# Prompt attention of an encoder layer: float32 steps on half of the array become float32r steps on the whole array

## The chip, the cores and the metric

One core of a Trainium2 chip runs the whole layer. The metric is device microseconds of one execution. TensorE (PE) multiplies; a weight load (PEld) comes ahead of every matmul. VectorE (DVE), ScalarE (ACT) and GpSimd (POOL) do the element-wise work, each from an in-order queue; SyncE (SP), ACT and POOL also issue DMAs.

## What is computed

The layer has a SwiGLU block, a mixer and a second SwiGLU block. The change lies in the mixer's attention over the 1024 prompt tokens: 16 query heads on 2 key heads, 64 wide; queries come in chunks of 64, and each chunk sees its own and the two earlier chunks (192 keys). A relative-position bias is added, and each head has a sink that joins the softmax without a value.

```python
s = jnp.einsum('...qhgd,...khd->...hgqk', q, k).astype(jnp.float32) * (HEAD_DIM ** -0.5) + bias
...
p = jax.nn.softmax(jnp.concatenate([s, sink_col], axis=-1), axis=-1)[..., :-1]
return jnp.einsum('...hgqk,...khd->...qhgd', p.astype(v.dtype), v)
...
merged = jax.nn.sigmoid(ga) * (attn @ w_ba) + jax.nn.sigmoid(gb) * (gm @ w_bg)
```

The attention of the 128 sample tokens (8 streams of 16) follows the same formula over cached keys.

## The kernel before

The 1152 tokens are nine tiles of 128, eight of the prompt and one of the samples. Everything runs over tiles 0 to 4 (block 0) and then tiles 5 to 8 (block 1). The large products (`mm3`, lines 254 to 256) split each float32 operand into hi (rounded to float32r) and lo (the rest) and take three float32r steps: hi·hi, hi·lo, lo·hi.

In the mixer, `project` makes queries, keys, values, gates and sigmoids; `attend` runs the attention with steps of another product between its pieces, the *filler*: `second`, the branch of the spatial gate (64 filler steps, each two `mm3`, so 384 float32r steps of half the block's tokens: 320 columns in block 0, 256 in block 1). After that `first` multiplies the attention's result with its weights and merges both branches; the output projection follows.

A *unit* of the attention is one pair of heads p (0 to 7, in the order `P_ORDER`) and one tile of 128 tokens: 8 x 5 = 40 units in block 0; 8 x 3 = 24 prompt units and 16 sample units in block 1. A unit has three parts. `scores`: two products of a pair's 128 query rows with 192 keys over the 64 rows of one head (line 1140, plain float32, 64 of 128 array rows), each followed on DVE by bias and running maximum (line 1143); a small row that bounds the maximum by the sink (1148); on ACT the exponentials with their sums (1151) and that of the sink (1153). `turn`: sum and reciprocal (1157, 1158), the division (1160, two rows), four transposes on PE (1166) and their copy from PSUM (1168, half on ACT, half on DVE). `values`: four float32 products that fill 64 of the 128 output rows each (1179); every two or three tiles the result is split into hi and lo (lines 264 and 265 of `put_split`). For each new unit's scores, the loop emits the turn of the second unit before it and the values of the third, with filler steps between; a scheduler then sets the order on each queue at build time. The weights of the filler are cut into hi (157, ACT) and lo (160, DVE), one pair per eight filler steps. The two halves of each of the filler's results are multiplied with a sigmoid that POOL loads from DRAM (`sig_load`), line 1300 on DVE.

## Time and profile before

| | us |
|---|---|
| median of 3 runs | 2617.04 (2615.02 to 2621.6) |
| span of the profiled execution | 2612.4 |
| PE busy | 2568.4 (98%) |
| DVE busy | 1885.8 (72%) |
| ACT busy | 1365.3 (52%) |
| POOL busy | 178.0 (7%) |
| share of PE in the chain that ended last | 91% |

The page's busy time is the time in which an engine has at least one instruction in flight. Neighbouring instructions of one engine overlap a little, so durations add up to more than busy time. A plain float32 product appears as two MATMUL records. "Idle before" is the engine's idle time just before the instructions of a group, with what ended it.

### The profile page before, as it was taken

To read this page: it belongs to the slowest core of one execution; us is meant where nothing else is said; L and a number is where in the kernel's file an instruction comes from. 1 tells how busy PE (TensorE), PEld (TensorE's weight loads), DVE (VectorE), ACT (ScalarE), POOL (GpSimd) and SP (SyncE) were. 2 spreads that over 40 slices of the span, in tenths; PEclk is the share of its full clock that TensorE was granted. 3 is DMA by queue.
4 is the path that set the end of the run, shared out by engine and by line. 5 is a ranking of instruction groups with operands and counts; after the bars stand their busy time and mean duration, and the time that the engine had idled before them with its cause. 6 is when DMAs were issued, how large, how long until landed. Compare 5 with 4: busy or idle time off the path is not lost.

```text
span 2612.4 us, 43405 instructions
## 1 busy us (share of the span) xinstructions
PE 2568.4 (98%) x16996; PEld 2349.2 (90%) x16996; DVE 1885.8 (72%) x3464; ACT 1365.3 (52%) x2575; POOL 178.0 (7%) x268
## 2 busy tenths in 40 slices
PE   6999999999999999999999999999999999999998
PEld 6999987999978999977989898797999987899986
DVE  6777664788877686666857877788876665688885
ACT  5444553555565555744446567545544454455552
POOL 1000000000210000100200201031000000000030
PEclk9999999999999999999999999999999999999999
DMA  4423322333443224412423444253332323333462
GB/s 123 97 82 97 114 95 95 118 113 98 163 144 116 82 90 148 126 56 65 167 86 113 127 147 132 71 179 120 108 95 81 97 89 109 126 99 113 129 209 81
DMA packets 216333, 293.92 MB, mean 113 GB/s; under 512 B 10824, under 2 KB 168880, under 8 KB 216128
## 3 DMA queue, kind: packets, MB, share of 16 engines
q1 hardware_dynamic: 183312, 212.36, 25.4%
q0 software_dynamic: 18048, 59.36, 7.6%
q10 hardware_dynamic: 14768, 19.43, 2.1%
q8 instruction: 133, 2.18, 0.3%
q14 instruction: 72, 0.59, 0.1%
HBM read 255.72 MB, written 35.39 MB: 111 GB/s over the span
## 4 chain that ended last, share of the span: by engine, by line
PE 91%; DVE 4%; DMA 2%; ACT 1%; issue 1%; SPq 0%; DVEq 0%; ACTq 0%
PE ps L254 28%; PE ps L255 28%; PE ps L256 28%; PE ps L1140 2%; PE ps L1179 2%; PE ps L1166 1%; PE ps L435 1%; DVE wl L160 1%; DMA wr<-in_w_in_dram 1%; DMA wr<-in_ffn_w_up_dram 1%; PE ps L1024 0%; DVE arena_r L265 0%; ACT wh L157 0%; DMA y<-w 0%; PE ps L962 0%
## 5 line engine op out<-in xcount | busy, mean ns | idle before, releaser
L254 PE MATMUL ps<-arena_r,wh 128*128 128x320 f32 (+1 forms) x4160 | 1244.1, 299 | 3.5 <-ACT arena_r L264 1.5
L256 PE MATMUL ps<-arena_r,wl 128*128 128x320 f32 (+1 forms) x4160 | 1229.2, 296 | 5.5 <-DVE wl L160 5.1
L255 PE MATMUL ps<-arena_r,wh 128*128 128x320 f32 (+1 forms) x4160 | 1230.8, 296 | 0.3 <-DVE arena_r L265 0.3
L254 PEld LDWEIGHTS ps<-arena_r,wh 128*128 128x128 f32 x4160 | 783.8, 188 | 16.6 <-issue 9.6
L256 PEld LDWEIGHTS ps<-arena_r,wl 128*128 128x128 f32 x4160 | 782.9, 188 | 11.9 <-DVE wl L160 7.4
L255 PEld LDWEIGHTS ps<-arena_r,wh 128*128 128x128 f32 x4160 | 783.7, 188 | 6.6 <-issue 5.0
L160 DVE TENSOR_TENSOR wl<-wr,wh 128x1024 fp32r<-128x1024 f32 x404 | 503.1, 1246 | 254.7 <-ACT wh L157 246.0
L157 ACT CAST wh<-wr 128x1024 fp32r<-128x1024 f32 x404 | 419.7, 1039 | 214.3 <-PE ps L255 178.8
L254 PE MATMUL ps<-wh,arena_r 128*128 128x512 f32 x936 | 374.9, 401 | 1.0 <-ACT arena_r L264 1.0
L255 PE MATMUL ps<-wl,arena_r 128*128 128x512 f32 x936 | 369.5, 395 | 0.0
L256 PE MATMUL ps<-wh,arena_r 128*128 128x512 f32 x936 | 369.0, 395 | 0.4 <-DVE arena_r L265 0.4
L264 ACT CAST arena_r<-arena 128x640 fp32r<-128x640 f32 (+4 forms) x246 | 158.9, 654 | 267.4 <-PE ps L255 220.3
L265 DVE TENSOR_TENSOR arena_r<-arena,arena_r 128x640 fp32r<-128x640 f32 (+4 forms) x246 | 186.7, 768 | 148.2 <-ACT arena_r L264 143.4
L256 PEld LDWEIGHTS ps<-wh,arena_r 128*128 128x128 f32 x936 | 175.4, 187 | 43.5 <-DVE arena_r L265 0.8
L254 PEld LDWEIGHTS ps<-wh,arena_r 128*128 128x128 f32 x936 | 175.5, 188 | 42.1 <-ACT arena_r L264 1.8
L255 PEld LDWEIGHTS ps<-wl,arena_r 128*128 128x128 f32 x936 | 175.7, 188 | 39.7
L541 DVE TENSOR_TENSOR t<-t,ps 128x320 f32<-128x320 f32 (+1 forms) x384 | 169.6, 446 | 46.1 <-PE ps L256 35.6
L160 DVE TENSOR_TENSOR wl<-arena,wh 128x1024 fp32r<-128x1024 f32 (+1 forms) x130 | 156.4, 1203 | 57.2 <-ACT wh L157 56.5
L545 ACT COPY t<-ps 128x320 f32<-128x320 f32 (+1 forms) x384 | 151.2, 396 | 81.4 <-PE ps L256 80.5
L157 ACT CAST wh<-arena 128x1024 fp32r<-128x1024 f32 (+1 forms) x130 | 134.6, 1035 | 111.2 <-PE ps L255 89.9
L597 ACT ACTIVATE t<-t 128x256 f32<-128x256 f32 (+1 forms) x129 | 57.3, 444 | 169.5 <-DVE t L541 169.4
L157 ACT CAST wh<-gn 128x1024 fp32r<-128x1024 f32 (+1 forms) x65 | 67.5, 1038 | 51.0 <-PE ps L255 42.3
(241 smaller groups left out, 2163.6 us busy)
## 6 DMA issues: line engine op xcount, KB each, us to landing
wr<-in_ffn_w_gate_dram SPq DMA_DIRECT2D x88, 512.0 KB, 4.0
wr<-in_ffn_w_up_dram SPq DMA_DIRECT2D x88, 512.0 KB, 5.0
wr<-in_w_in_dram SPq DMA_DIRECT2D x84, 512.0 KB, 4.9
wr<-in_ffn_w_down_dram SPq DMA_DIRECT2D x40, 1024.0 KB, 5.0
y<-w ACTq DMA_DIRECT2D x38, 256.0 KB, 3.4
arena<-x POOLq DMA_DIRECT2D x19, 512.0 KB, 4.2
arena<-y POOLq DMA_DIRECT2D x17, 512.0 KB, 5.2
x<-arena POOLq DMA_DIRECT2D x16, 512.0 KB, 3.0
```

The costliest lines, as they stand in the source:

```text
L157: nc.scalar.copy(out=self.hi, in_=self.src)
L160: nc.vector.tensor_tensor(out=self.lo, in0=self.src, in1=self.hi.bitcast(F32), op=ALU.subtract)
L254: nc.tensor.matmul(out, lh, rh, start=start, stop=False, skip_group_check=again)
L255: nc.tensor.matmul(out, lh, rl, start=False, stop=False, skip_group_check=again)
L256: nc.tensor.matmul(out, ll, rh, start=False, stop=stop, skip_group_check=again)
L264: nc.scalar.copy(out=hi, in_=src)
L265: nc.vector.tensor_tensor(out=lo, in0=src, in1=hi.bitcast(F32), op=ALU.subtract)
L541: nc.vector.tensor_tensor(out=out, in0=a, in1=b, op=ALU.add)
L545: nc.scalar.copy(out=t, in_=ps)
L597: nc.scalar.activation(out=t, in_=v, func=AF.Silu)
L1140: nc.tensor.matmul(sc, self.q[p % 4][hp, 2 * mi + c].rearrange("p e q -> p (e q)"), k_all[hp, k1 - n:k1], start=True, stop=True)
L1179: nc.tensor.matmul(po[64 * e:64 * e + 64, c0:c0 + P], v_t[:, m - 1 + a, hp], pt[:, a, :, 64 * e:64 * e + 64], start=(a == a0), stop=(a == 1))
```

## The change

Scores and values of the prompt units become float32r steps that use all 128 rows and columns.

- The keys of one head are split into hi and lo, each laid on both halves of the partitions (`keys`, twice per block). The queries of a pair lie as hi on one half and lo on the other (`queries`, once per pair): ACT copies 64 rows, DVE subtracts 64 rows. One step over 128 rows then gives (hi + lo of the queries) times hi of the keys, a second step the same with lo.
- The values lie as hi and lo side by side (128 columns). The transposed probabilities are split with `put_split` into hi (ACT) and lo (DVE), 512 columns each. Four float32r steps of 256 columns give the product with hi in 64 output rows and with lo in the other 64; for each tile ACT copies one half (64 x 256) and DVE adds the halves in two rows (64 x 128).
- Scores are kept negated (queries scaled by -1/8, bias table negated), the running minimum starts at the negated sink, a per-partition column, and the small bounding row goes away. The division is one two-operand row over both chunks (384 columns) in place of two rows of 192, except in tile 0.
- The attention's result is kept in float32 where the spatial gate's part of the merge was kept; that part goes to DRAM over ACT's DMA queue and comes back with the sigmoids in `first` (four loads per feature tile in place of two). All splits of the attention's result come after it, six of them between filler steps.
- The filler steps ahead of the attention and after it are 10 and 8 in place of 6 and 6; `P_ORDER` begins with pair 4.

```diff
+        def keys(self, h):
+            mine, other = (slice(64 * e, 64 * e + 64) for e in (h, 1 - h))
+            src = k_all[mine, self.t0 * P:(self.t0 + self.n_k) * P]
+            hi, lo = self.kr[h]
+            for rows in (mine, other):
+                nc.scalar.copy(out=hi[rows], in_=src)
+            for rows in (mine, other):
+                nc.vector.tensor_tensor(out=lo[rows], in0=src, in1=hi[mine].bitcast(F32), op=ALU.subtract)
+            put_split(self.vr[h][:, :, 0:64], self.vr[h][:, :, 64:128],
+                      v_t[:, self.t0:self.t0 + self.n_k, mine])
+        def queries(self, p):
...
+            nc.scalar.copy(out=t[mine], in_=src)
+            nc.vector.tensor_tensor(out=t[other], in0=src, in1=t[mine].bitcast(F32), op=ALU.subtract)
...
-                    nc.tensor.matmul(sc, self.q[p % 4][hp, 2 * mi + c].rearrange("p e q -> p (e q)"),
-                                     k_all[hp, k1 - n:k1], start=True, stop=True)
-                    seg = pb[:, c, j1 - n:j1]
+                    for a in range(2):
+                        nc.tensor.matmul(sc, qt[:, 2 * mi + c, :], self.kr[h][a][:, k1 - n:k1],
+                                         start=a == 0, stop=a == 1)
+                    seg = pc[:, c, j1 - n:j1]
                     nc.vector.tensor_tensor_reduce(out=seg, in0=sc, in1=bias_of(p)[:, 192 - n:192],
-                                                   scale=1.0, scalar=NEG, op0=ALU.add, op1=ALU.max,
-                                                   accum_out=s[:, c:c + 1])
+                                                   scale=1.0, scalar=nsink_p[:, p:p + 1], op0=ALU.add,
+                                                   op1=ALU.min, accum_out=s[:, 2 + c:3 + c])
                     segs.append(seg)
                 nm = s[:, 2:4]
-                nc.vector.tensor_scalar(out=nm, in0=s[:, 0:2], scalar1=sink, scalar2=-1.0,
-                                        op0=ALU.max, op1=ALU.mult)
...
+                    nc.vector.tensor_tensor(out=both, in0=both, op=ALU.mult,
+                                            in1=rc.unsqueeze(2).broadcast_to([P, 2, 192]))
...
-                for a in range(a0, 2):
-                    (nc.vector.tensor_copy if a else nc.scalar.copy)(out=pt[:, a], in_=ps[:, a])
+                put_split(ph[:, a0:], pl[:, a0:], ps[:, a0:])
...
-                    for e in range(2):
-                        nc.tensor.matmul(po[64 * e:64 * e + 64, c0:c0 + P],
-                                         v_t[:, m - 1 + a, hp], pt[:, a, :, 64 * e:64 * e + 64],
-                                         start=(a == a0), stop=(a == 1))
+                    for pt in (ph, pl):
+                        nc.tensor.matmul(po[:, i * 256:(i + 1) * 256], self.vr[h][:, m - 1 - self.t0 + a, :],
+                                         pt[:, a, :], start=a == a0 and pt is ph, stop=a == 1 and pt is pl)
+                if i == 1 or mi == self.n_p - 1:
+                    for j in range(i + 1):
+                        t = tmp(256)
+                        nc.scalar.copy(out=t[0:64], in_=po[64:128, j * 256:(j + 1) * 256])
...
+                            nc.vector.tensor_tensor(out=out.rearrange("p (n q) -> p n q", q=64),
+                                                    in0=v[0][:, :, e], in1=v[1][:, :, e], op=ALU.add)
...
-                nc.vector.tensor_tensor(out=self.gm[f][:, j * self.w:(j + 1) * self.w], in0=sig, in1=ps,
-                                        op=ALU.mult)
+                nc.vector.tensor_tensor(out=sig[0], in0=sig[0], in1=ps, op=ALU.mult)
+                nc.scalar.dma_start(out=sig_d[1][f][:, j * self.w:(j + 1) * self.w], in_=sig[0])
...
+            for p in P_ORDER[:6]:
+                put_split(*self.attn[p], self.attn_f[p])
+                step()
             run(filler)
-            for p in self.held:
-                put_split(*self.attn[p], self.held[p])
+            for p in P_ORDER[6:]:
+                put_split(*self.attn[p], self.attn_f[p])
...
-    blocks_[0].attend(blocks_[0].second(), 6, 6)
+    blocks_[0].attend(blocks_[0].second(), 10, 8)
```

How the queues change is shown at two places of block 0. In the names, `st` is a unit's column of sums, `w` its scores and probabilities, `ps` a PSUM bank, `gn` the transposed probabilities (after: their hi), `arena_87` float32 and `arena_r_88` float32r places.

DVE before, in the middle of block 0's attention: the units of `st_11612`, `st_11643` and `st_11676`.

```order
L1143 ISA w_10731,st_11643<-ps_11644,arena_87 128x64 [waits PE_49]
L1143 ISA st_11643 128x1
L1143 ISA w_10731,st_11643<-ps_11644,arena_87 128x128 [waits PE_49]
L1157 TENSOR_TENSOR st_11612<-st_11612 128x2 [waits Activation_49]
L1148 TENSOR_SCALAR st_11643<-st_11643,sink_p_124 128x2 [waits DVE_49]
L1158 RECIPROCAL st_11612<-st_11612 128x2 [waits DVE_49]
L1160 TENSOR_SCALAR w_10730<-w_10730,st_11612 128x192 [waits DVE_49]
L1160 TENSOR_SCALAR w_10730<-w_10730,st_11612 128x192
L1157 TENSOR_TENSOR st_11643<-st_11643 128x2 [waits Activation_49]
L1143 ISA w_10732,st_11676<-ps_11677,arena_87 128x192 [waits PE_49]
L1143 ISA st_11676 128x1
L1168 COPY gn_10733<-ps_11663 128x256 [waits Activation_49]
```

The sum of a unit (1157) stands behind its bias rows and the rows of another unit, and a copy of 256 columns ends the unit's turn.

DVE after, in the middle of block 0's attention (units `st_11663`, `st_11698`, `st_11728`; line 1188 is the bias row, 1200 and 1201 sum and reciprocal, 1207 the division, 265 the lo part of the transposed probabilities).

```order
L1188 ISA w_10736,st_11698<-ps_11699,arena_87,nsink_p_126 128x192 [waits PE_49]
L1188 ISA st_11698 128x1
L1207 TENSOR_TENSOR w_10735<-w_10735,st_11663 128x2x192 [waits DVE_49]
L1200 TENSOR_TENSOR st_11698<-st_11698 128x2 [waits Activation_49]
L1201 RECIPROCAL st_11698<-st_11698 128x2 [waits DVE_49]
L1207 TENSOR_TENSOR w_10736<-w_10736,st_11698 128x2x192 [waits DVE_49]
L265 TENSOR_TENSOR arena_r_88<-ps_11718,gn_10737 128x512 [waits Activation_49]
L1188 ISA w_10734,st_11728<-ps_11729,arena_87,nsink_p_126 128x192 [waits PE_49]
L1188 ISA st_11728 128x1
L265 TENSOR_TENSOR arena_r_88<-ps_11748,gn_10737 128x512 [waits Activation_49]
```

The small bounding row is gone, the division is one row, the copy of 256 columns has become a subtraction of 512, and the sum of unit `st_11698` stands one row behind that unit's last bias row.

PE before, in block 0: the end of one unit, the scores of another, and filler.

```order
L1140 MATMUL ps_11757<-arena_87 128x192 [waits DVE_49]
L1166 MATMUL ps_11776<-ident_89,w_10732 128x128 [waits DVE_49] x2
L1166 MATMUL ps_11776<-ident_89,w_10732 128x128 x2
L1179 MATMUL ps_11783<-gn_10733,arena_87 64x128 [waits PE_49]
L1179 MATMUL ps_11783<-gn_10733,arena_87 64x128
L1140 MATMUL ps_11787<-arena_87 128x192
L254 MATMUL ps_11714<-arena_r_88,wh_11279 128x320
L255 MATMUL ps_11714<-arena_r_88,wh_11279 128x320
L256 MATMUL ps_11714<-arena_r_88,wl_11280 128x320
```

Each score call is one plain float32 product over 64 rows, and filler steps follow it.

PE after, in block 0 (1217 the transposes, 1228 the values, 1185 the scores).

```order
L1217 MATMUL ps_11718<-ident_89,w_10734 128x128 [waits DVE_49,PE_49]
L1217 MATMUL ps_11718<-ident_89,w_10734 128x128 [waits Activation_49]
L1217 MATMUL ps_11718<-ident_89,w_10734 128x128 x2
L1228 MATMUL ps_11725<-gn_10737,arena_r_88 128x256 [waits Activation_49]
L1228 MATMUL ps_11725<-arena_r_88 128x256
L1185 MATMUL ps_11729<-arena_r_88 128x192 [waits PE_49]
L1185 MATMUL ps_11729<-arena_r_88 128x192
L1217 MATMUL ps_11748<-ident_89,w_10735 128x128 [waits DVE_49,Activation_49]
L1217 MATMUL ps_11748<-ident_89,w_10735 128x128 [waits Activation_49]
L1217 MATMUL ps_11748<-ident_89,w_10735 128x128 x2
L1228 MATMUL ps_11725<-gn_10737,arena_r_88 128x256 [waits Activation_49]
```

Each score call is now two float32r steps on the whole array, and the value steps wait for ACT (hi) and, for the steps with lo, for DVE.

## Rows read from the trace of the kernel before

**Rows 1.** Windows: stretch, us, busy (count) of PE, PEld, DVE, ACT, POOL; clock, DMA, GB/s
```profile
1060.00:1101.20 41.20, 41.20 (x282) 41.03 (x280) 28.72 (x34) 34.31 (x58) 6.24 (x11) 1.00 0.51 154
1101.20:1244.70 143.50, 143.50 (x924) 103.87 (x924) 95.84 (x434) 68.50 (x256) 10.20 (x19) 1.00 0.20 65
1244.70:1300.00 55.30, 55.30 (x378) 55.30 (x379) 46.12 (x101) 23.58 (x48) 18.86 (x21) 1.00 0.48 161
1602.20:1683.60 81.40, 81.40 (x552) 58.79 (x552) 58.61 (x256) 42.57 (x149) 4.28 (x8) 1.00 0.19 60
1683.60:1730.20 46.60, 46.01 (x414) 38.86 (x414) 32.47 (x141) 22.22 (x101) 10.56 (x30) 1.00 0.31 101
```

**Rows 2.** Groups of PE, block 0's attention: count, busy us, mean ns, idle before
```profile
L254 PE MATMUL ps<-arena_r,wh 128*128 128x320 f32 x111 | 39.9, 359 | 0.0
```

**Rows 3.** The same view, block 1's prompt units
```profile
L254 PE MATMUL ps<-arena_r,wh 128*128 128x256 f32 x67 | 21.4, 319 | 0.0
```

**Rows 4.** Timeline of PE in block 0: start us, length us, instructions
```profile
1099.82 0.31 PE L254 MATMUL ps<-arena_r,wh 128*128 128x320 f32 x1
...
1100.99 0.31 PE L256 MATMUL ps<-arena_r,wl 128*128 128x320 f32 x1
...
1103.04 0.31 PE L256 MATMUL ps<-arena_r,wl 128*128 128x320 f32 x1
1103.28 0.59 PE L1140 MATMUL ps<-arena 64*128 64x192 f32 x2
1103.80 0.41 PE L254 MATMUL ps<-arena_r,wh 128*128 128x320 f32 x1
1104.05 0.31 PE L255 MATMUL ps<-arena_r,wh 128*128 128x320 f32 x1
...
1169.25 0.66 PE L1166 MATMUL ps<-ident,w 128*128 128x128 f32 x4
1169.66 0.39 PE L254 MATMUL ps<-arena_r,wh 128*128 128x320 f32 x1
```

**Rows 5.** Groups of DVE, block 0's attention: count, busy us, mean ns, idle before
```profile
L1143 DVE CUSTOM_DVE_ANT_0 w<-ps,arena 128x192 f32<-128x192 f32 x64 | 22.8, 356 | 22.7 <-PE ps L1140 21.9
L1160 DVE TENSOR_SCALAR w<-w,st 128x192 f32<-128x192 f32 x64 | 18.5, 316 | 0.7
L1148 DVE TENSOR_SCALAR st<-st,sink_p 128x2 f32<-128x2 f32 x40 | 8.9, 224 | 0.1
L160 DVE TENSOR_TENSOR wl<-wr,wh 128x1024 fp32r<-128x1024 f32 x7 | 8.5, 1216 | 0.0
L1300 DVE TENSOR_TENSOR arena<-t,ps 128x320 f32<-128x320 f32 x14 | 6.6, 484 | 1.2 <-PE ps L256 0.8
L1157 DVE TENSOR_TENSOR st<-st 128x2 f32<-128x2 f32 x40 | 6.2, 155 | 2.6 <-ACT st L1153 2.5
L265 DVE TENSOR_TENSOR arena_r<-ps,arena_r 128x384 fp32r<-128x384 f32 x6 | 3.3, 548 | 0.0
L1160 DVE TENSOR_SCALAR w<-w,st 128x64 f32<-128x64 f32 x8 | 2.0, 251 | 0.1
L265 DVE TENSOR_TENSOR arena_r<-arena,arena_r 128x640 fp32r<-128x640 f32 x1 | 0.8, 817 | 0.0
```

**Rows 6.** The same view, block 1's attention
```profile
L265 DVE TENSOR_TENSOR arena_r<-ps,arena_r 128x128 fp32r<-128x128 f32 x4 | 1.1, 285 | 0.4 <-ACT arena_r L264 0.4
```

**Rows 7.** Timeline of ACT and DVE in block 0
```profile
1168.24 0.45 ACT L1151 ACTIVATE w<-w,st 128x192 f32<-128x192 f32 x1
1168.27 0.88 DVE L1300 TENSOR_TENSOR arena<-t,ps 128x320 f32<-128x320 f32 x2
...
1168.68 0.28 ACT L1153 ACTIVATE st<-st,sink_p 128x2 f32<-128x2 f32 x1
```

**Rows 8.** Windows in other stages, where PE has idle time (columns as in Rows 1)
```profile
1490.00:1500.00 10.00, 7.36 (x54) 7.15 (x53) 7.23 (x9) 4.75 (x8) 0.00 (x0) 0.88 0.76 260
1780.00:1790.00 10.00, 7.73 (x37) 5.81 (x35) 9.26 (x28) 6.78 (x11) 0.73 (x2) 1.00 0.62 211
```

More of the change, by code (lines that the diff above doesn't have):

```diff
@@ L1155, in turn @@
+                nc.scalar.activation(out=s[:, 6:8], in_=nm, func=AF.Exp, bias=sink_p[:, p:p + 1])
             def turn():
-                dn = s[:, 8:10]
+                dn, rc = s[:, 8:10], s[:, 10:12]
                 nc.vector.tensor_tensor(out=dn, in0=s[:, 4:6], in1=s[:, 6:8], op=ALU.add)
-                nc.vector.reciprocal(out=s[:, 10:12], in_=dn)
-                for c in range(2):
-                    nc.vector.tensor_scalar(out=segs[c], in0=segs[c], scalar1=s[:, 10 + c:11 + c],
-                                            scalar2=None, op0=ALU.mult)
@@ L1162, in turn @@
-                ps = bank().rearrange("p (a c t) -> p a c t", a=2, c=2)
+                nc.vector.reciprocal(out=rc, in_=dn)
+                if m > 0:
+                    flat = pb[:, 0:192].unsqueeze(1)
+                    both = bass.AP(tensor=flat.tensor, offset=flat.offset,
+                                   ap=[flat.ap[0], [320, 2], [1, 192]])
+                    nc.vector.tensor_tensor(out=both, in0=both, op=ALU.mult,
+                                            in1=rc.unsqueeze(2).broadcast_to([P, 2, 192]))
+                else:
+                    for c in range(2):
+                        nc.vector.tensor_scalar(out=segs[c], in0=segs[c], scalar1=rc[:, c:c + 1],
+                                                scalar2=None, op0=ALU.mult)
@@ L1236, in values @@
                     for g in range(4):
-                        put_split(*(v[:, self.n_p * P:].rearrange("p (b q) -> p b q", b=8)
-                                    for v in self.attn[4 * h + g]), src[:, g])
+                        (nc.vector.tensor_copy if g % 2 else nc.scalar.copy)(
+                            out=self.attn_f[4 * h + g][:, self.n_p * P:].rearrange("p (b q) -> p b q", b=8),
+                            in_=src[:, g])
             return scores, turn, values
@@ L1266, in sig_load @@
         def sig_load(self, a, f):
-            ts = [tmp(self.w) for _ in range(2)]
+            ts = [tmp(self.w) for _ in range(2 if a else 4)]
             for j, t in enumerate(ts):
-                nc.gpsimd.dma_start(out=t, in_=sig_d[a][f][:, j * self.w:(j + 1) * self.w])
+                nc.gpsimd.dma_start(out=t, in_=sig_d[a if j < 2 else 1][f][:, j % 2 * self.w:(j % 2 + 1) * self.w])
             return ts
@@ L1290, in branch @@
                         for j in range(2):
-                            done(f, j, sig[j], ps[j])
+                            done(f, j, sig[j::2], ps[j])
                     yield
@@ L1333, in attend @@
             step(lead)
+            self.keys(1)
+            self.queries(P_ORDER[0])
             rate, due = (KT * KT - lead - rest) / (2.0 * len(units)), 0.0
```

81 lines of the change are left out of this document (50 added, 31 removed).

## The prediction

> **What bounds the kernel now.** I read the windows first, stage by stage, since the mean shares mix stages. In block 0's attention, 1101.20 to 1244.70, PE is busy 143.50 of 143.50 us, DVE 95.84, ACT 68.50; in block 1's prompt units, 1602.20 to 1683.60, PE 81.40 of 81.40, DVE 58.61; in the sample units PE 46.01 of 46.60 [rows 1]. So PE sets all three, and what DVE does is hidden. Next the groups of PE and its timeline, for the price of the attention's PE work. A float32r step of 320 columns starts .146 us after its neighbour (from 1099.82 to 1100.99, eight steps) [rows 4]; by columns, one of 256 costs .117 and one of 192 about .09. Block 0's stretch holds 3 x 111 less one, 332, filler steps [rows 2]: 48.5 us. The other 95.0 are 40 units of 2.38. Block 1's prompt stretch holds 3 x 67 plus one, 202 [rows 3]: 23.6, which leaves 57.8, or 2.41 for each of 24 units. One score call takes about .72 in the stream, .52 of it its own and the rest lost at both changes from filler (.24 ahead, .25 behind, against .146) [rows 4]; four transposes take .41 [rows 4].
>
> **PE's part of the change.** A full unit becomes four score steps, four transposes and four value steps. No float32r step of 192 columns is in the trace. Bounds: .09 by columns, and .26, half of a score call's .52 [rows 4]; I take .10, near the float32r rows, the same kind of operation on the same 128 rows. 4 x .10 + .41 + 4 x .117 = 1.28; a unit of tile 0 (narrower keys, two transposes, two value steps) .83. Filler moves as well: by the order 315 steps stand between block 0's first and last scores and 167 between block 1's, since more of them are held for the start and end. Block 0: 32 x 1.28 + 8 x .83 + 315 x .146 = 93.6; block 1: 24 x 1.28 + 167 x .117 = 50.2. The steps that leave the stretch are still done, so I compare with 143.5 - 17 x .146 = 141.0 and 81.4 - 35 x .117 = 77.3. PE alone would save 47.4 and 27.1.
>
> **DVE's part.** That gain isn't had if another queue is longer. In DVE's queue a row costs its duration less about .08, the overlap of neighbours (two rows of .484 take .88 [rows 5, 7]). The rows of after, for each:
> - Bias row: .356 [rows 5]. It now reads a per-partition column instead of a constant; the bounding row, which reads one, lasts .224, the sum on the same 128x2 without one .155 [rows 5]. I take +.07 (bounds 0 and .07): .35 in the queue, .25 for tile 0's narrow ones.
> - Sum and reciprocal: .31 together, from .155 each, little overlapped [rows 5].
> - Division as one two-operand row of 384. The two-operand row L265 takes .285 for 128 and .548 for 384 columns [rows 5, 6], 1.05 ns a column: .55, .47 in the queue. The two old rows cost 2 x (.316 - .08) = .47 [rows 5]: nothing gained. Their slope, from .251 at 64 and .316 at 192 [rows 5], is only .51 ns.
> - lo of the transposed probabilities: .548 + 128 x 1.05 = .68, so .60 (.33 in tile 0), in place of half of a copy.
> - Two sums of halves per tile, .205 each (as L265 with 128 columns).
> - Queries: a subtraction of 1280 columns, 1.40 by the slope from .817 at 640 [rows 5]; in block 1 of 768, .87. Filler: L1300's successor .40 (.33), L160 1.14, a split of the attention's result .74 [rows 5].
>
> The Trainium skill (VectorE: DVE Perf Modes, section "Mode 2×_2P — use both read ports for one tensor") says that a one-source operation in on-chip memory can do two elements a cycle, which one with two operands cannot. It speaks against merging the divisions, and the two slopes, 1.05 and .51 ns, agree; at the faster rate the merged row would be .13 shorter, and the sum 7 us lower.
>
> Block 0, first to last bias row, counted in the order: bias rows 32 x .70 + 8 x .50 = 26.4; sums and reciprocals 39 x .31 = 12.1; divisions 31 x .47 + 8 x .37 = 17.5; lo 29 x .60 + 7 x .33 = 19.7; 70 sums of halves 14.4; 6 queries 8.4; 10 products 4.0; 5 L160 5.7; 3 splits 2.2. Together **110.4**, more than PE's 93.6: DVE is the bound. ACT, 68.50 before [rows 1], would come to 106 if its added pieces cost 40 x (.60 + .35); it stays below.
>
> Waits come on top. Behind a unit's last bias row come the second exponential (.44 from its start to the small one's), the small one (.28) [rows 7] and DVE's own .08: .80. Where the sum stands one row behind (the division, .47, between), DVE waits .33; about one unit in five stands so, 2.6 us. I double it, since bias rows also wait for PE, whose transposes wait for DVE: 5.5 (bounds: 0, and 40 x .80 = 32). Filling and emptying the pipeline: 1.5 and 5. Block 0: **122.4**, a saving of 141.0 - 122.4 = 18.6.
>
> Block 1's prompt units by the same prices: 16.8 + 6.8 + 10.3 + 12.6 + 7.8 + 5.2 + 2.0 + 3.4, and 1.6 for copies of cached keys, 66.5; waits 3.3, filling 1.5: **71.3**. Saving 6.0. The sample units keep their operations, and PE stays their bound (46.01 of 46.60, DVE 32.47 [rows 1]): 0.
>
> **Around the stretches.** Ahead of the first scores the split keys and first queries put about 6 us each on ACT and DVE, in the order of five subtractions of 1280 columns. Before, ACT was busy 34.31 and DVE 28.72 of 41.20 us there [rows 1], under PE's steps, which are now four more; most is hidden, I take 1 us a block (bounds 0 and 4). Behind the attention, eight splits per block lie between filler steps, and sixteen more sigmoid tiles are loaded by POOL, busy 18.86 of 55.30 there [rows 1]: 0, with 8 a block if `first` had to wait for them.
>
> Sum: 18.6 + 6.0 - 2 = 22.6. The profiled span is 2612.4, the median 2617.0 lies 4.6 above; 2617.0 - 22.6 = **2594**.
>
> **Rivals.**
> A, the above: .60. Its own range is 2584 (no waits) to 2606 (waits three times as long).
> B, DVE lighter: the column operand is free (128 x .07 = 9.0) and nothing waits (8.8). Against it: L1148's .224. 2594 - 18 = 2576; .12.
> C, narrow float32r steps cost .26: block 0's PE comes to 117.3, block 1's to 65.6. PE and DVE are then about even and each waits for the other; with waits doubled 117.3 + 11 + 6.5 = 134.8 and 66.5 + 6.6 + 1.5 = 74.6, a saving of 6.2 + 2.7 - 2 = 7: 2610; .09. Against it: .146 per filler step on the same rows.
> D, the engines take turns: each unit's sum waits the whole .80 behind its last bias row, because DVE has nothing else ready. That adds 64 x .80 - 8.8 = 42: 2636, **slower**. It decides from 22.6 / 64 = .35 us of further waiting a unit. For it: after L1160 DVE's order is short of rows that depend on nothing; against: the order puts another unit's work behind the bias rows in four of five. .10.
> E, DVE doesn't bind and PE's sum alone counts: 47.4 + 27.1 - 2, 2545; .02. The Trainium skill (TensorEngine Tiling (Array Packing), section "PSUM Bottleneck") warns that after a speedup of TensorE the copies out of PSUM may become the bottleneck; no row of before shows it, as PE was full. By that warning the time is A's, without it E's.
> F, `first` waits 8 us a block for its added loads: 2611; .04.
> G, PE, now some 77% busy, loses clock. In a window at 7.36 of 10 the granted clock was .88, in one at 7.73 it was 1.00 [rows 8]. At .88 PE's 93.6 become 106, still below DVE; only at .75 on the mean (125 and 67) does PE set the end: about 2602; .03.
>
> **How the numbers follow.** The likeliest is A, 2594. From 2575 to 2618 all of A, C, F and G and most of B are held; D and E are left out. About 0.3%, 7.9 us, is what a measurement here can tell from no change: same is 2609 to 2625, which takes F, half of C and A's end, .11; slower is D, .10; faster .79.
>
> **What would show it.** Block 0's stretch from first to last scores near 122 us and block 1's near 71, with DVE busy over 90% of it and PE well below full; PE's idle time ended by DVE or ACT. Bias rows of 192 at .42 (at .36 B is right), the division .55, lo with 512 columns .68, the sums of halves .285. Score steps .09 to .11 apart in the stream (.26: C). Idle time ahead of the sum near .1 a unit on the mean (.8: D). `first` waiting on no transfer (else F), clock 1.00 (else G). The prediction is wrong if DVE is idle for more than a tenth of the stretch while PE is idle too.

## The result and the profile after

The changed kernel takes 2633.15 us (median of 4 runs, 2628.4 to 2634.42) against 2617.46 before: ratio 1.0055, 95% interval 1.0041 to 1.0069. It is slower by 15.7 us, where 23 us less were forecast, with a range of 2575 to 2618.

The page of after, busy time and chain that ended last:

```profile
PE 2537.3 (96%) x16756; PEld 2359.5 (90%) x16756; DVE 1951.2 (74%) x3476; ACT 1425.1 (54%) x2661; POOL 194.1 (7%) x300
...
PE 81%; DVE 9%; ACT 4%; DMA 3%; issue 2%; POOL 0%; SPq 0%; ACTq 0%; DVEq 0%; POOLq 0%
```

PE's busy time fell by 31 us, as meant, and its share of the chain from 91% to 81%: PE now waits. Where, the windows tell (columns as in [rows 1]). The first row is block 0's attention from the first score step to the last value step, the second the part of it from first to last bias row, the third block 1's prompt units from first to last score step, the fourth its sample units, the fifth a piece of these.

```profile
1106.20:1246.80 140.60, 116.33 (x767) 102.96 (x766) 126.89 (x441) 99.42 (x298) 8.57 (x16) 0.96 0.25 82
...
1108.70:1237.20 128.50, 106.35 (x697) 93.87 (x698) 115.42 (x417) 93.75 (x287) 8.04 (x15) 0.96 0.22 75
...
1610.30:1686.40 76.10, 61.31 (x439) 54.61 (x437) 69.97 (x243) 54.90 (x166) 4.83 (x9) 0.96 0.23 73
1686.40:1745.40 59.00, 53.45 (x381) 46.76 (x379) 36.40 (x133) 25.27 (x102) 10.09 (x29) 0.74 0.24 74
...
1695.60:1726.20 30.60, 29.02 (x159) 25.85 (x160) 13.74 (x59) 9.53 (x43) 3.24 (x11) 0.50 0.25 78
```

Three things are to be seen against [rows 1]. PE, which was full, is idle for 24 of 140.6 us in block 0. DVE is the fullest engine, at 90%. And the sample units, whose operations hardly changed, take 59.0 us where before, between the same marks, they took 46.5, with the granted clock at .74; for 30.6 us it was .50 (1.2 GHz) although PE was busy 29.02 of them.

Both programs run the same 15288 float32r steps of the large products in the same order, so the start of the n-th such step can be compared. Block 0's attention, with what stands close around it (steps 6680 to 7120, 1097.0 to 1256.7 before), gained 0.9 us. Block 1's entry lost 1.2 (to step 9460), its prompt and sample units lost 14.3 (to step 9900, 1740.8 before and 1757.4 after). The rest, 3.3 us in sum, lies in small pieces elsewhere, 1.6 of them ahead of block 0's attention.

The groups of DVE in block 0's attention after (columns as in [rows 5]):

```profile
L1188 DVE CUSTOM_DVE_ANT_0 w<-ps,arena,nsink_p 128x192 f32<-128x192 f32 x64 | 26.1, 411 | 1.2 <-PE ps L1185 0.6
L265 DVE TENSOR_TENSOR arena_r<-ps,gn 128x512 fp32r<-128x512 f32 x32 | 22.0, 687 | 2.0 <-ACT gn L264 1.6
L1238 DVE TENSOR_TENSOR arena<-ps,t 64x128 f32<-64x128 f32 x78 | 21.8, 280 | 1.8 <-ACT t L1233 0.9
L1207 DVE TENSOR_TENSOR w<-w,st 128x384 f32<-128x384 f32 x32 | 17.7, 554 | 0.5
L1159 DVE TENSOR_TENSOR arena_r<-arena,arena_r 64x1280 fp32r<-64x1280 f32 x6 | 8.9, 1486 | 1.4 <-ACT arena_r L1158 1.2
...
L1200 DVE TENSOR_TENSOR st<-st 128x2 f32<-128x2 f32 x40 | 5.9, 155 | 3.2 <-ACT st L1196 3.1
```

The prices are those of the prediction: bias row .411 (.42 forecast), lo .687 (.68), division .554 (.55), queries 1.486 (1.48). Before, DVE's idle time stood ahead of the bias row, with PE as its releaser ([rows 5], 22.7 us); now that is 1.2. The wait has changed sides, as PE's waits show (who waited for whom, us in total, times, longest):

```profile
ACT w L1194 <- DVE st L1188: 20.4, 31, 1.6
PEld ps L1185 <- DVE st L1188: 16.9, 23, 2.6
...
PE ps L1185 <- DVE st L1188: 11.4, 17, 2.4
```

PE's *score steps* (1185) wait for DVE's *bias row* (1188), which reads what score steps wrote. A stretch of the timeline shows how (start, length; in brackets the idle time ahead):

```profile
1143.38 0.45 PE L1185 MATMUL ps<-arena_r 128*128 128x192 f32 x2
1143.45 1.22 DVE L160 TENSOR_TENSOR wl<-wr,wh 128x1024 fp32r<-128x1024 f32 x1
...
1144.58 0.68 DVE L265 TENSOR_TENSOR arena_r<-ps,gn 128x512 fp32r<-128x512 f32 x1
...
1145.18 0.57 DVE L1238 TENSOR_TENSOR arena<-ps,t 64x128 f32<-64x128 f32 x2
1145.79 0.42 DVE L1188 CUSTOM_DVE_ANT_0 w<-ps,arena,nsink_p 128x192 f32<-128x192 f32 x1
...
1146.27 0.74 PE L1185 MATMUL ps<-arena_r 128*128 128x192 f32 x2 [2.44 <-DVE st L1188]
```

The code issues the first chunk's score steps, its bias row, then the second chunk's steps, which write the same PSUM bank. So the second pair of steps waits until DVE, busy with work of other units, has come to the first chunk's bias row, and everything behind it on PE waits too. The wait was there before as well (the second product of 1140 "waits DVE" in the order); it cost nothing while DVE was ahead. The Trainium skill (PSUM — Partial Sum Buffer, section "PSUM bank collisions raise a hardware error") says why it can't just be dropped: TensorE may not write a bank that another engine is reading; no run here shows that.

### The profile page after: what moved, and what is told of

Same layout as the page of the kernel before. It is cut to its first block, busy times and chain, and to the rows that moved or that the text cites. A ratio compares the mean times of both kernels' runs of the same rounds, so it can differ in the third digit from the quotient of the medians.

```text
span 2630.4 us, 43244 instructions
## 1 busy us (share of the span) xinstructions
PE 2537.3 (96%) x16756; PEld 2359.5 (90%) x16756; DVE 1951.2 (74%) x3476; ACT 1425.1 (54%) x2661; POOL 194.1 (7%) x300
## 4 chain that ended last, share of the span: by engine, by line
PE 81%; DVE 9%; ACT 4%; DMA 3%; issue 2%; POOL 0%; SPq 0%; ACTq 0%; DVEq 0%; POOLq 0%
PE ps L254 26%; PE ps L256 26%; PE ps L255 26%; DVE wl L160 1%; DVE arena_r L265 1%; DMA wr<-in_w_in_dram 1%; PE ps L435 1%; DVE w L1188 1%; DMA wr<-in_ffn_w_up_dram 1%; DVE arena L1238 1%; ACT wh L157 1%; DMA y<-w 1%; ACT w L1194 0%; PE ps L1039 0%; DVE w L1207 0%
## 5 line engine op out<-in xcount | busy, mean ns | idle before, releaser
L160 DVE TENSOR_TENSOR wl<-wr,wh 128x1024 fp32r<-128x1024 f32 x404 | 508.1, 1258 | 249.7 <-ACT wh L157 240.7
L264 ACT CAST arena_r<-arena 128x640 fp32r<-128x640 f32 (+4 forms) x264 | 169.3, 651 | 266.8 <-PE ps L255 215.7
L265 DVE TENSOR_TENSOR arena_r<-arena,arena_r 128x640 fp32r<-128x640 f32 (+4 forms) x264 | 196.5, 754 | 145.1 <-ACT arena_r L264 140.1
L199 DVE TENSOR_TENSOR arena<-wr 128x1024 f32<-128x1024 f32 (+1 forms) x65 | 78.4, 1206 | 26.8 <-DMA wr<-in_w_in_dram 12.3
```

Of the source, the lines that this page charges most:

```text
L160: nc.vector.tensor_tensor(out=self.lo, in0=self.src, in1=self.hi.bitcast(F32), op=ALU.subtract)
L199: nc.vector.tensor_tensor(out=out, in0=x, in1=y, op=op)
L264: nc.scalar.copy(out=hi, in_=src)
L265: nc.vector.tensor_tensor(out=lo, in0=src, in1=hi.bitcast(F32), op=ALU.subtract)
```

## The experiments

The theory after the result: (1) waits between PE and DVE, chiefly the one above, stretch the prompt units beyond DVE's own work; (2) the gaps they leave on PE let its clock fall, which costs most in the sample units. The rivals are named in each expectation. "Stretch" is block 0's attention from first score to last value step. Each run is compared with the kernel before on the same chip. Every edit makes the scheduler set the order on the queues anew, so a run changes more than its own lines.

| kernel | us (median) | ratio to before, 95% | stretch, us | samples, us |
|---|---|---|---|---|
| before | 2617.46 | | 143.4 | 46.5 |
| after | 2633.15 | 1.0041 to 1.0069 | 140.6 | 59.0 |
| e1_seam | 2629.01 | 1.0027 to 1.0053 | 140.3 | 47.6 |
| e2_poolsub | 2628.80 | 1.0017 to 1.0048 | 147.4 | 44.9 |
| e3_scores_only | 2593.81 | .9881 to .9920 | 122.6 | 43.3 |
| e4_values_only | 2664.64 | 1.0154 to 1.0195 | 159.2 | 59.2 |
| e5_warm | 2693.11 | 1.0272 to 1.0305 | 178.9 | 55.0 |
| e6_no_sums | 2600.71 | .9914 to .9950 | 125.8 | 43.8 |
| e7_pairs | 2619.18 | .9995 to 1.0014 | 135.5 | 49.7 |
| e8_scores_pairs | 2578.09 | .9837 to .9874 | 114.2 | 46.7 |
| e9_before_pairs | 2600.17 | .9908 to .9938 | 131.1 | 46.0 |
| e10_values_pairs | 2629.65 | 1.0017 to 1.0043 | 146.3 | 47.6 |
| e11_two_div | 2620.03 | .9996 to 1.0020 | 135.2 | 57.6 |
| e12_pairs_no_sums | 2599.39 | .9909 to .9942 | 125.1 | 46.8 |

**e1_seam: work in the gap ahead of the sample units.** The gap is this one in the timeline of after:

```profile
1693.03 1.23 DVE L160 TENSOR_TENSOR wl<-wr,wh 128x1024 fp32r<-128x1024 f32 x1
...
1694.37 0.69 DVE L265 TENSOR_TENSOR arena_r<-ps,gn 128x512 fp32r<-128x512 f32 x1
1694.98 0.57 DVE L1238 TENSOR_TENSOR arena<-ps,t 64x128 f32<-64x128 f32 x2
...
1695.78 0.36 DVE L1258 CUSTOM_DVE_ANT_0 t<-ps,arena,nsink_s 128x144 f32<-128x144 f32 x1
...
1697.18 0.66 PE L1274 MATMUL ps<-ident,w 128*128 128x128 f32 x2 [3.25 <-ACT st L1265]
```

The bias row of a sample unit (1258) stands behind the last prompt units' rows on DVE; the transposes (1274) wait for it through ACT.

```diff
+            held = 6 if self.b == 1 else 0
-            rate, due = (KT * KT - lead - rest) / (2.0 * len(units)), 0.0
+            rate, due = (KT * KT - lead - rest - held) / (2.0 * len(units)), 0.0
...
+                if held and u in (n_prompt + 1, n_prompt + 2):
+                    step(held // 2)
```

> As the changed kernel, but in block 1 six filler steps (36 float32r steps) are held back and done at the passage from the prompt units to the sample units, ahead of the first sample transposes. Theory: 17 us of the loss are TensorE's clock. In the changed kernel's trace PE stood idle 3.25 us at that passage, the granted clock then fell to 0.50 and stayed there for some 30 us, through most of the sample units. With work in the gap the clock stays at 1.00, the sample units take 46 us again, and the time is 2633 - 16 = 2617 us (2612 to 2621). Rival: the sample units are longer for their own reasons (three places instead of four for the transposed probabilities, fewer filler steps between them); then only the gap itself is saved, 3 us at most: 2629 to 2634.

The samples' window:

```profile
1695.50:1743.10 47.60, 44.09 (x402) 38.48 (x401) 35.44 (x130) 24.33 (x101) 9.76 (x27) 1.00 0.30 89
```

Clock 1.00, and 47.6 us for 152 filler steps (records of lines 254 to 256) where after took 59.0 for 126: with the 26 steps (3.0 us) set off, 14.4 us less, of which the gap itself was 3.25. That the clock makes the sample units long, holds. In e2_poolsub too, where the clock happened to hold at this place (.96), the samples took 44.9, and in e6_no_sums, with the sample units' code of after and 133 filler steps, 43.8 at clock 1.00. The whole gained 4 us only, and the two intervals overlap: the time is the rival's (2629 to 2634). By the n-th filler step, as above, the profiled execution gained 12.7 us in the sample units and lost 4.5 in block 1's prompt units, where the steps now missing left gaps (their window is 78.6 long, clock .91). Another 5.9 were lost ahead of block 1's attention, where PE has the same steps in the same order; profiled executions differ by that much in such places. Nor do six held steps keep the clock up for sure: in e5_warm, which has them too, the samples took 55.0.

**e2_poolsub: the queries' subtraction on POOL.**

```diff
-            nc.vector.tensor_tensor(out=t[other], in0=src, in1=t[mine].bitcast(F32), op=ALU.subtract)
+            nc.gpsimd.tensor_tensor(out=t[other], in0=src, in1=t[mine].bitcast(F32), op=ALU.subtract)
```

> As the changed kernel, but the subtraction that makes lo of the queries is on POOL instead of DVE (eight per block, 1.49 us each on DVE in block 0, .95 in block 1). Theory: DVE's queue sets the length of the prompt stretches. Six of the eight lie inside each stretch, so block 0's stretch (first score to last value step, 140.6 us) falls by 9 to about 132, block 1's first to last score by about 5 from 76; the time falls by about 14, to 2619, if the clock at the samples does as before. Rival: not DVE's amount of work but the chain of waits between the engines sets it; then under 3 us are saved, 2630 to 2634, or the time grows because POOL's subtraction ends late.

The time, 2628.8, lies between both expectations. The stretch grew to 147.4, and DVE's busy time in it from 126.9 to 132.3 although it lost 8.9 us of rows: the sums (1200) alone rose from 5.9 to 15.9. One place of its timeline, POOL and DVE:

```profile
1123.20 2.91 POOL L1159 TENSOR_TENSOR arena_r<-arena,arena_r 64x1280 fp32r<-64x1280 f32 x1 [15.12 <-ACT arena_r L1158]
...
1123.96 2.17 DVE L1200 TENSOR_TENSOR st<-st 128x2 f32<-128x2 f32 x1
```

A sum of two columns, .155 otherwise, lasts 2.17 and ends with POOL's row. So the edit did not take the work off DVE, and the run tells nothing on the theory. The Trainium skill (SBUF — State Buffer, section "SBUF: two separate sides") says that VectorE, with two inputs in that memory, and GpSimd lock one port pair against each other for a whole instruction; the row agrees.

**e3_scores_only and e4_values_only: each half of the change alone.** e3 takes back the values and e4 the scores; the rest of the change (the division, the spatial gate's part over DRAM, the filler's places) stays in both:

```diff
-                put_split(ph[:, a0:], pl[:, a0:], ps[:, a0:])
+                for a in range(a0, 2):
+                    (nc.vector.tensor_copy if a else nc.scalar.copy)(
+                        out=pt[:, a], in_=ps[:, a].rearrange("p (c t) -> p c t", c=2))
...
+                    for e in range(2):
+                        nc.tensor.matmul(po[64 * e:64 * e + 64, c0:c0 + P],
+                                         v_t[:, m - 1 + a, hp], pt[:, a, :, 64 * e:64 * e + 64],
+                                         start=(a == a0), stop=(a == 1))
```

```diff
-                    for a in range(2):
-                        nc.tensor.matmul(sc, qt[:, 2 * mi + c, :], self.kr[h][a][:, k1 - n:k1],
-                                         start=a == 0, stop=a == 1)
+                    nc.tensor.matmul(sc, self.q[p % 4][hp, 2 * mi + c].rearrange("p e q -> p (e q)"),
+                                     k_all[hp, self.t0 * P + k1 - n:self.t0 * P + k1], start=True, stop=True)
```

> Only the scores are float32r steps; the transposed probabilities are copied, half on ACT and half on DVE, and the values are plain float32 steps on 64 of the columns, as in the kernel before; ACT copies each result of two or three tiles. Theory (DVE binds after the change): DVE loses the lo rows (.60 each in the queue) and the sums of halves (two of .28 per tile) and gets half copies (.34): some .8 us less a unit, block 0's stretch holds about 85 us of DVE. PE has 143.5 less 80 x .45 less 15 filler steps, about 105, so PE binds again, at 110 to 118: 2617 - 25 - 12 = about 2580 (2570 to 2592), clock 1.00. Rival: the chain of waits binds whatever DVE's work: block 0's stretch stays over 130, the time over 2605.

> Only the values are float32r steps with hi and lo; the scores are the plain float32 products of the kernel before, on the unsplit queries and keys. Theory: DVE has some 107 us in block 0's stretch without the queries' subtractions; PE has 143.5 less 32 units x .2 less 15 filler steps, about 135: PE binds at 136 to 140, with few gaps, the clock stays at 1.00 and the time is about 2612 to 2618, as before the change. Rival: the part with the values is what makes the waits, whatever the scores cost; then PE's share in the stretch stays below 90% and the time is over 2625.

The window of e3's stretch, and those of e4's, of its samples and of a piece of its stretch:

```profile
1108.70:1231.30 122.60, 117.28 (x894) 94.59 (x893) 98.45 (x360) 81.95 (x267) 11.25 (x21) 1.00 0.29 98
```

```profile
1105.10:1264.30 159.20, 147.05 (x752) 115.52 (x752) 117.48 (x431) 91.20 (x292) 8.58 (x16) 0.87 0.22 72
...
1721.30:1780.50 59.20, 55.10 (x368) 46.54 (x367) 35.24 (x132) 24.60 (x101) 11.16 (x31) 0.71 0.28 90
1139.80:1163.70 23.90, 21.49 (x69) 16.22 (x69) 13.37 (x44) 8.37 (x27) 0.54 (x1) 0.50 0.23 72
```

Against the kernel before on their chip (2619.35) the scores alone gain 26 us, with PE nearly full and the clock 1.00; time and stretch lie a little above the theory's 2592 and 118. The values alone lose 45, and the theory for e4 fell: its rival, over 2625, is right. Its clock was .87 in the stretch and .71 in the samples. A gap of 2.87 us on PE ends at 1140.7; from 1139.8 to 1163.7 the clock stays at .50 with PE busy 21.49 of 23.90 on transposes, plain float32 scores, float32r values and filler.

**e5_warm: added work for PE.** Ahead of each unit's scores eight float32r steps write columns of the unit's bank that nobody reads (on top of e1_seam).

```diff
+                for _ in range((8, 8)[self.b]):
+                    nc.tensor.matmul(ps[:, 384:512], self.vr[h][:, 0, :], self.vr[h][:, 1, :], start=True, stop=True)
```

> As e1_seam, with eight float32r steps of 128 columns more ahead of each prompt unit's scores, whose results nobody reads; they only keep TensorE busy in both prompt stretches. Theory: the half clock costs the prompt stretches time too (10 us of block 0's stretch and 14 of block 1's ran at half clock in e1_seam). With the clock at 1.00 block 0's stretch falls from 140.3 to about 135, block 1's from 78.6 to about 73, and the time to about 2617. Rival: the half clock in the prompt stretches hides behind DVE and the added steps cost PE .5 us a unit; then the stretches stay or grow and the time is 2627 to 2640.

It is slower by 64 us than e1_seam, more than the rival allowed. Two lines of PE's timeline, and the group of the score steps in the stretch:

```profile
1182.45 1.00 PE L1180 MATMUL ps<-arena_r 128*128 128x128 f32 x8
1183.29 0.41 PE L1187 MATMUL ps<-arena_r 128*128 128x192 f32 x2
```

```profile
L1187 PE MATMUL ps<-arena_r 128*128 128x192 f32 x128 | 29.2, 310 | 18.9 <-DVE st L1190 18.9
```

The eight steps take .84 us (.105 each, so a step of 128 columns costs no less than one of 192). The stretch grew by 38.6 us, .97 a unit, though PE had .6 idle a unit and was busy only 150.8 of 178.9. Work put into PE's idle time did not fill it; it lengthened the loop. That fits two engines that wait for each other in turn: if the first score steps come .84 later, so does DVE's bias row, and the second score steps behind it. On the clock in the prompt units the run says nothing.

**e6_no_sums: less for DVE.**

```diff
-                        t = tmp(256)
-                        nc.scalar.copy(out=t[0:64], in_=po[64:128, j * 256:(j + 1) * 256])
...
+                            nc.scalar.copy(out=out.rearrange("p (n q) -> p n q", q=64), in_=v[:, :, e])
```

> As the changed kernel, but the sums of the two halves of the values are left out: ACT copies the half with hi of the values in two pieces, DVE has no row for it (the part with lo of the values is left out of the result). Theory: the amount of DVE's work sets the prompt stretches. DVE loses 22 of 127 us in block 0's stretch and 13 of 70 in block 1's: 140.6 falls to about 120, 76.1 to about 65, and with fewer gaps on PE the clock stays up at the samples: about 2590 (2582 to 2602). Rival: waits between PE and DVE set them, whatever DVE's amount: block 0's stretch stays over 132, the time over 2612.

```profile
1105.40:1231.20 125.80, 107.70 (x757) 96.69 (x757) 106.88 (x363) 102.28 (x337) 11.25 (x21) 1.00 0.30 99
```

20 us less on DVE shorten the stretch by 14.8, and the clock stays at 1.00. So DVE's amount counts; the time is in the theory's range, the stretch above its 120. But at 125.8 no engine is fuller than 86%: something else sets the rest. PE's wait for the bias row is as long as in the changed kernel (11.4 there), though DVE now has idle time:

```profile
PE ps L1185 <- DVE st L1188: 10.9, 20, 1.8
```

**e7_pairs: the second score step no longer behind the first bias row.**

```diff
                     for a in range(2):
                         nc.tensor.matmul(sc, qt[:, 2 * mi + c, :], self.kr[h][a][:, k1 - n:k1],
                                          start=a == 0, stop=a == 1)
+                for c in range(2):
+                    n = 192 if m > 0 else (64, 128)[c]
+                    j1 = (192, 256)[c]
+                    sc = ps[:, c * 192:c * 192 + n]
                     seg = pc[:, c, j1 - n:j1]
```

> As the changed kernel, but a unit's four score steps are issued together, ahead of both bias rows. In the changed kernel the steps of the second chunk stand behind the first chunk's bias row, in the same PSUM bank, and wait for it, so PE stops until DVE's queue comes to that row: the longest of PE's waits (11.4 us in block 0's stretch, with 20 us of ACT behind the same row). Theory: this wait makes most of PE's gaps; without it block 0's stretch falls from 140.6 to 125 to 132, block 1's from 76.1 to about 70, there is little half clock, and the time is about 2600 (2590 to 2612). Rival: DVE's amount of work sets the stretches, the gaps only move to another step of PE: block 0's stretch stays at 136 or more, the time over 2620.

Window of the stretch, and the longest of PE's own waits in it:

```profile
1104.90:1240.40 135.50, 110.88 (x768) 102.88 (x767) 125.19 (x441) 97.72 (x298) 8.57 (x16) 0.96 0.26 86
```

```profile
PE ps L1221 <- DVE w L1211: 12.4, 13, 2.5
```

14 us are gained, 5.1 of them in the stretch and 9.3 in the sample units (59.0 to 49.7, clock .74 to .95; what this part is worth, e11 shows). The stretch falls between the two expectations, the time just under the rival's 2620. The wait of the score steps is gone, and as much stands now ahead of the transposes (1221), for DVE's division (1211). DVE, at 125.2 of 135.5, is nearly full.

**e8_scores_pairs: both findings together,** e3 with e7's order.

> e3_scores_only (float32r scores alone) with the score steps of a unit issued together as in e7_pairs. PE was busy 117.3 of 122.6 us in block 0's stretch and 62.4 of 68.2 in block 1's. Theory: what idle time there was came from the same wait; the stretches fall to about 118.5 and 64, the time from 2594 to about 2586. Rival: nothing changes, 2592 to 2596, as PE is the bound there already.

```profile
1104.40:1218.60 114.20, 109.84 (x893) 92.45 (x891) 97.64 (x360) 78.44 (x267) 11.22 (x21) 1.00 0.31 104
1582.10:1643.40 61.30, 57.61 (x507) 48.19 (x506) 53.39 (x199) 42.39 (x147) 4.81 (x9) 1.00 0.28 90
```

2578.09 us, 1.4% under the kernel before (interval 1.3 to 1.6%) and the fastest of all. It fell twice as far as expected: PE's busy time also shrank, from 117.3 to 109.8. A part of that is the same wait, which the busy time hides, as it runs to the modelled end of the step ahead: in e3's stretch a score step starts right behind a filler step 32 times, .34 us after it on the mean, in e8's 3 times, .145 after it. One such place in e3:

```profile
1145.69 0.39 PE L254 MATMUL ps<-arena_r,wh 128*128 128x320 f32 x1
1146.15 0.47 PE L1183 MATMUL ps<-arena_r 128*128 128x192 f32 x2
```

The rest was not split.

**e9_before_pairs: the order alone,** the same edit in the kernel before.

> The kernel before, with a unit's two score products issued together, ahead of both bias rows. There PE has no idle time to lose in the prompt stretches (143.4 of 143.4 us busy), though the second product waits for the first bias row as well. Theory: the order alone saves PE only changes between filler and plain float32 products, of which some 50 of 64 in block 0 stand between the two products of a unit, .19 us each: 2617 - 4 to 12 = 2605 to 2613, so most of the 41 us by which e8_scores_pairs beats the kernel before belong to the float32r scores. Rival: no change, 2614 to 2620; or, against both, the order is worth what it was worth between e3 and e8 (16 us): 2600.

```profile
1105.70:1236.80 131.10, 131.10 (x924) 104.25 (x924) 92.83 (x434) 68.42 (x255) 10.21 (x19) 1.00 0.22 71
```

19 us, more than the theory's 4 to 12, and the time of the second rival: PE is full as before but does the same work in 131.1 instead of 143.4. Block 0 has 40 such pairs (not 64, as the expectation counted), so the order is worth .31 a pair. In the traces of the two stretches a score product comes right behind a filler step 35 times before and 2 times here: .37 for each filler between that is gone, twice the .19 of the theory. Each against the kernel before on its own chip, e8 gains 40 us and the order alone 19; the other 21 belong to the float32r scores with the rest of the change.

**e10_values_pairs,** e4 with the same order.

> e4_values_only (float32r values, plain float32 scores; 2665 us, 41 of 159 us of block 0's stretch and 61 of 153 in block 1 at half clock) with a unit's score products issued together. Theory: e4's loss is the half clock, begun by gaps that come of the wait of the second score product for the first bias row; PE's own work there was about 147 - 20 = 127 us. Without that wait the half clock stays under 15 us in each block and the time is 2605 to 2630. Rival: DVE's work with the values makes gaps in another place, the clock falls as before: over 2640.

```profile
1104.90:1251.20 146.30, 134.14 (x758) 115.03 (x758) 116.53 (x431) 89.54 (x292) 8.62 (x16) 0.88 0.24 79
```

The time came as the theory said, 2629.65, but for another reason: half clock did not go below 15 us in a block (.88 in the stretch of 146.3 is 35 us at half), only the samples came back to 47.6 at a higher clock. With float32r values PE has gaps in either order.

**e11_two_div: the division as two one-operand rows,** in e7.

```diff
-                    nc.vector.tensor_tensor(out=both, in0=both, op=ALU.mult,
-                                            in1=rc.unsqueeze(2).broadcast_to([P, 2, 192]))
+                for c in range(2):
+                    nc.vector.tensor_scalar(out=segs[c], in0=segs[c], scalar1=rc[:, c:c + 1],
+                                            scalar2=None, op0=ALU.mult)
```

> e7_pairs with the division as two one-operand rows of 192 columns, as in the kernel before, in place of one two-operand row of 384. Theory of the prediction: 2 x (.316 - .08) = .47 against .47 in DVE's queue, no difference: 2616 to 2622. Rival: the merged row is really the cheaper one, since each row has a wait of its own for the one before: 64 units x .1 slower, about 2626. Other rival: the one-operand rows are cheaper: 2612.

2620.03 against e7's 2619.18: no difference, as priced. The windows of the sample units, in e11 and in e7:

```profile
1680.40:1738.00 57.60, 54.43 (x386) 46.88 (x384) 37.05 (x139) 25.88 (x103) 10.35 (x29) 0.76 0.23 75
```

```profile
1681.10:1730.80 49.70, 46.31 (x390) 39.05 (x388) 36.64 (x137) 25.71 (x104) 10.64 (x30) 0.95 0.36 107
```

The profiled executions of two kernels with the same median stand 8 us apart at this one place, by the clock: of such kernels the medians are to be compared, not the profiles. The ten runs of e11 form two groups by clock, and show what a fall costs in one and the same kernel: four with a mean granted clock of .985 to .989 took 2625.67 to 2628.83 us, the profiled one among them; six with .992 or .993 took 2615.40 to 2620.70. All ten runs of e7 have .992 to .994, all four of after .986 to .990. By these groups some 8 of e7's 14 us are the clock at the samples and the others the order in the prompt units.

What brings the fall about, part (2) of the theory, is not shown. Here it came, for 27.3 us, without a long gap: in the 14 us ahead of it PE was never idle for more than .60 us at a time. The windows just ahead and of the fall:

```profile
1686.00:1690.90 4.90, 3.75 (x24) 2.83 (x23) 4.36 (x13) 3.03 (x10) 0.85 (x5) 1.00 0.28 71
1690.90:1718.20 27.30, 27.30 (x147) 24.12 (x145) 12.68 (x55) 8.80 (x43) 4.20 (x13) 0.50 0.24 80
```

And in e10 a gap of 2.1 us at the same passage (to 1703.4) was followed by 36 us at clock 1.00.

**e12_pairs_no_sums: are the wait and DVE's amount two causes?**

> e6_no_sums and e7_pairs together (the part with lo of the values is left out of the result). If DVE's amount of work and the wait of the second score step are two separate causes, their savings in block 0's stretch add: 140.6 - 14.8 - 5.1 = 121, block 1 likewise, and the time is 2601 - 14 = about 2587 (2581 to 2593). If they are one cause seen twice (the wait is only where DVE's length shows), the time is that of e6_no_sums, 2597 to 2603.

```profile
1107.10:1232.20 125.10, 106.71 (x752) 97.89 (x751) 107.23 (x363) 99.88 (x337) 11.26 (x21) 0.99 0.30 96
```

2599.39 and 125.1, the same as e6: the savings don't add, as the second expectation has it. Its reason is not shown by that. PE's waits in the stretch stand now at the value steps (1232), for lo (265, DVE) and hi (264, ACT):

```profile
PE ps L1232 <- DVE arena_r L265: 10.8, 16, 0.9
PE ps L1232 <- ACT gn L264: 5.0, 11, 0.7
```

A wait that is taken away comes back at the next step of the same chain. Either the wait of the score steps was only DVE's lateness, one cause seen twice, or something else holds 125 us and hides the second saving. What holds 125 us with PE, DVE and ACT each at 80 to 86% is not settled. The part that e6 and e12 have and e3 and e8 lack is the chain of the values (transposes, hi on ACT, lo on DVE from the same bank, four steps, ACT's copies); a run with one more unit in flight, which would show it, was not tried, since it needs more places for scores and probabilities.

## Why the prediction was wrong

- **DVE becomes the bound:** right. Every price of a row came within 3% but one: the two sums of halves of a tile take .57 together (1145.18 in the timeline), not 2 x .205. That is the 5 us by which DVE is busier between first and last bias row, 115.4 against 110.4.
- **Waits, 5.5 us in block 0:** the step that failed. In that part DVE was idle 13.1. With 2.5 ahead of the first bias row (1.5 forecast) and 9.6 from the last one to the last value step (5 forecast), 140.6 stands in place of 122.4: 18.2 us over, 5.0 by amount, 7.6 by waits, 5.6 at the ends. Without the wait of the score steps 5.1 come back (e7). The waits were read off DVE's order alone, at the sum (1200), where they are indeed small (3.1 us). That PE's second score step waits behind DVE's bias row could be read in the rows of the order ("waits DVE"), and was passed over, since PE had no idle time there before. The upper end of A's own range, 2606 for waits three times as long, is also misadded: 2594 + 2 x 8.8 is 2612. The sign set for being wrong, DVE idle for over a tenth of the stretch, hardly showed: 13.7 of 140.6.
- **PE's part, 93.6 us:** the score steps cost about what was taken where none waits, here .20 for two (the steps of a pair in e8 start .11 apart), as the timeline of after shows:

```profile
1163.34 0.36 PE L1185 MATMUL ps<-arena_r 128*128 128x192 f32 x2
1163.54 0.33 PE L254 MATMUL ps<-arena_r,wh 128*128 128x320 f32 x1
```

  PE was busy 116.3 all the same; some 5 us of that are half clock, and busy time runs to the modelled end of the last instruction ahead of each gap; it was not split further. The 315 filler steps reach to the last value step (317 counted there), not to the last score as the text said.
- **Sample units, 0:** wrong by 12.5 us between their own marks, with 20 filler steps fewer between them, and this turned a lost gain into a loss. The clock was weighed as rival G, but for the prompt stretches alone, where PE had time to spare. Nobody asked what a fallen clock costs in the next stretch, which PE does bound: 30.6 us at .50. Some 8 us of it depend on whether the clock falls in the execution (e11).
- **Block 1's prompt units:** 76.1 against 71.3; with the filler steps moved, 1.2 us gained where 6.0 were forecast, by the same waits.
- **Entry 1 us a block, exit 0:** right (0 and 1.2; under 1 us).
- **Rivals:** D, the engines taking turns, gave 2636 and the measured time is near it, by luck: its place was wrong (the sum's wait behind ACT, 3.1 us in block 0), and 12.5 us of the loss are the samples' clock. But e5 fits turns of that kind, between score step and bias row. C, F and G as priced did not happen, nor E. B is refuted by the bias row, .411.

That the two halves of the change pull against each other was in no rival: the scores gain 26 us alone (e3), the values lose 45 alone (e4) and, with the better order, 41 on top of the scores (e7 against e8) or 29 on top of plain ones (e10 against e9). For PE the values bring little: the plain products took about .53 of a unit's 2.38 (less two score calls of .72 and .41 of transposes, [rows 2, 4]), the four float32r steps take .47 at the filler's price, while DVE pays .60 for lo and .57 a tile for the sums in place of half a copy.

## What to carry to other kernels

When a change frees a full engine, look at every wait of that engine on the next fullest one, also those that cost nothing so far: the order shows them, the trace of before doesn't. Price the two halves of a change by the engine that will bind afterwards, and apart from each other; here the scores save PE a microsecond a unit for little DVE and are the gain, the values save it a tenth at most, pay with most of a microsecond of DVE, and are the loss. And ask of every new gap on TensorE what the stretch behind it would take at half clock.

## What the runs showed of the hardware

- With a gap on PE of 2.87 us (e4, to 1140.7) and one of 3.25 (after, to 1697.2) the granted clock fell to .50 and stayed there for 23.9 and 30.6 us, PE busy nine tenths of them and more, in stretches where plain float32 attention steps stand between the float32r ones. The Trainium skill (TensorE: Matmul & The Clock Gate, section "HAM oscillation — how this bites in real kernels") tells that gaps throttle TensorE; these two falls agree. Why it fell in e11 with no gap over .60 us just ahead, and why it stays low so long under work, none of these runs explains.
- Changes between plain float32 on half the array and float32r on the whole of it may cost more than the .19 read off one place of the trace for a score call's two changes: keeping two score products together saved 12.3 us in block 0's stretch of the kernel before (e9), .31 for each of 40 pairs; how much of it is the changes themselves was not split.
- A POOL row of 2.91 us held up a DVE row of two operands, .155 otherwise, until its end (e2).
- A float32r step of 128 columns takes .105 (e5, eight in .84), one of 192 .10 (after, two in .20): with a weight load ahead of every step (.19 each in the trace), the narrower one is not cheaper.
